# One core of a Trainium2: scales, rotated key and latents prepared in the merge, a query and key stage in a written order, and longer waits in the plan of a delta rule

## The chip, the cores and the metric

The kernel runs on one core of a Trainium2 chip. Its time is the device time of one execution in microseconds (us). A core has TensorE (PE, matrix products), VectorE (DVE), ScalarE (ACT), GpSimd (POOL) and SyncE (SP), each with a queue of its own that is worked off in order, and 16 DMA engines that move data between memory (HBM) and the core's SBUF. TensorE writes its products to PSUM.

## The reference

One layer of a diffusion trunk over 1024 tokens of width 1024 and 256 context tokens. A projection `h @ w_in` feeds three branches: a Fourier mix, a gated delta rule (4 heads, in both directions, in chunks) and attention with low-rank queries and keys (MLA, 8 heads); gates merge them. Cut to the parts that the change touches:

```python
# delta rule, one step of the scan over chunks
u_new = u_n - einsum('bhcd,bhde->bhce', w_n, S)
o = einsum(qg_n, S) + einsum(qk_n, u_new)
S = S * gl_n + einsum('bhcd,bhce->bhde', kd_n, u_new)
...
# MLA: 384 query latents cq, 256 key/value latents ckv, 32 key channels kpe
q = (rmsnorm(cq, q_norm) @ w_uq).reshape(B, L, 8, 64 + 32)
kv = (rmsnorm(ckv, kv_norm) @ w_ukv).reshape(B, L, 8, 64 + 64)
q_pe = apply_rope(q_pe, cos, sin);  kpe = apply_rope(kpe, cos, sin)
q = concatenate([q_nope, q_pe]);    k = concatenate([k_nope, k_pe for each head])
o = softmax(q @ k.T * 96 ** -0.5) @ v
...
merged = sum over a, b, c of sigmoid(g) * (y @ w_branch);  y = merged @ w_out
x = x + gate * rmsnorm(y, g_post)
```

## The kernel before

Values are float32. Where TensorE needs them, an operand is split into a high and a low half (names ending in h and l, or hi and lo), and a product is three matmuls: high x high, low x high, high x low. ScalarE writes the high half, VectorE or POOL the low one.

The stages follow one another, with the times of the profiled execution: a prologue (0 to 155 us), the delta rule over the context (to 330), the Fourier branch (to 427), the delta rule over the tokens (`gdn_lat`, to 985), the merge (`merge_ab`: gates to 1047, then a loop over eight output blocks m to 1139), the query and key stage (`qkv`, 1139 to 1240), attention (`attend`, to 1491) and the end (`final`).

In `gdn_lat` a planner, `drive`, mixes three kinds of generators: `prep` (the inverse of a head's chunk matrices: the 16 x 16 blocks are inverted by a chain of VectorE products and reductions `tmp`, `N`, L746 and L748, stored to `zd` and loaded as `Z`), `scan` (eight steps per head with S, y and u) and *fillers*, which are projections that other stages need later (`mm<-hhi,wh` and the like). A chain that yields a number says for how many us, times PAD = 1.25, it will wait; the planner issues filler pieces of three matmuls until that time is up by its own costs. With `self.fine` set, matmuls stay in the order in which the code issues them. Small functions put on `self.later` run inside a filler: `mla_scales` (the tokens' inverse norms, stored as `rkd` and `aqd`) and `rope_k` (the key channels `kped` times the table `ropek`, stored as `kpd`).

In the merge loop a block has 48 matmuls `pb` of 512 columns; VectorE multiplies them with gate values `t` (L1266). `ck_prep`, called after block 5, splits the key latents into `ckh`, `ckl` and the value weights into `wvh`, `wvl`. The gates' sum `gacc` runs over weights `in_wmod` that SP loads.

`qkv` computes from the latents: `k_tile(t)` and `qn_tile(t)` (keys and queries, PSUM tile `st`, stored by halves as `knh`, `knl`, `qnh`, `qnl`), `qp_tile` (rotated query channels, `qph`, `qpl`), `v_tile` (`acc`). Weights come by SP (`wr`, L209), are split into `wh` and `wl`. `load_k` and `load_q` bring the stored halves back as `K` and `Q` in the layout of attention. `peak` multiplies a tile of K and Q (`s`) and takes row maxima on VectorE (`mx`), which `shift` turns into the softmax's shift. The scheduler is free to interleave these.

Of the kernel before, what the change touches and what calls it, by code (L numbers as in the profile page):

```python
# [162 lines left out]
class K:  # L163
# [89 lines left out]
    def build(self):  # L253
        with ExitStack() as es:
# [27 lines left out]
            self.kpd = dr.tile([32, L], FP32, name="kpd")  # L282
# [38 lines left out]
            with tc.tile_pool(name="pre", bufs=1, side="right", reuse_waits="tile") as self.pre:  # L321
                self.merge_ab()
                esh.close()
                esq = ExitStack()
                self.qk = esq.enter_context(tc.tile_pool(name="qk", bufs=1, reuse_waits="tile"))
                self.pss = esq.enter_context(tc.tile_pool(name="pss", bufs=1, space=PSUM, reuse_waits="tile"))
                self.qkv()
            self.kq = es.enter_context(tc.tile_pool(name="kq", bufs=1, side="right", reuse_waits="tile"))
# [341 lines left out]
    def gdn_prep(self, kap, qap, gsl, bsl, h=0):  # L670
# [165 lines left out]
    def gdn_step(self, st, c, S, kap, ktok, vtok, M, bkc, eg, eL, lat, last, al):  # L836
# [129 lines left out]
    def gdn_lat(self):  # L966
# [16 lines left out]
        def scan(h, kT, qT, ktok, vtok, bk, M, Qf):  # L983
# [3 lines left out]
            for t in range(8):  # L987
# [7 lines left out]
                yield 0.8  # L995
# [45 lines left out]
    def fillers(self):  # L1041
# [3 lines left out]
        self.later.append(self.mla_scales)  # L1045
        self.later.append(self.rope_k)
# [57 lines left out]

    def mla_scales(self):
        nc, gp = self.nc, self.gp
        rk = gp.tile([P, 10], FP32, name="rk")
        nc.vector.tensor_scalar(out=rk, in0=self.ssk, scalar1=1.0 / 256, scalar2=EPS, op0=ALU.mult, op1=ALU.add)
        self.ipow(self.rkv, rk, -0.5)
        self.rkd = self.dram.tile([10, P], FP32, name="rkd")  # L1110
        nc.sync.dma_start(out=self.rkd.rearrange("t p -> p t"), in_=self.rkv, allow_slow_non_contiguous=True)
        rq = gp.tile([P, 8], FP32, name="rq")
        nc.vector.tensor_scalar(out=rq, in0=self.ssq, scalar1=96.0 / 384, scalar2=96 * EPS, op0=ALU.mult, op1=ALU.add)
        self.ipow(self.aq, rq, -0.5)
        self.aqd = self.dram.tile([8, P], FP32, name="aqd")
        nc.sync.dma_start(out=self.aqd.rearrange("t p -> p t"), in_=self.aq, allow_slow_non_contiguous=True)

    def rope_k(self):
        nc, gp = self.nc, self.gp

        def st():
            return gp.tile([P, 512], FP32, name="st", bufs=self.nb["st"])

        for b in range(0, L, 512):
            k, r, t = st(), st(), st()
            nc.sync.dma_start(out=k[0:64], in_=self.kped[:, b:b + 512])
            nc.sync.dma_start(out=r[0:64], in_=self.a["ropek"][:, b:b + 512])
            nc.gpsimd.tensor_tensor(out=k[0:64], in0=k[0:64], in1=r[0:64], op=ALU.mult)
            nc.scalar.copy(out=t[0:32], in_=k[32:64])
            nc.gpsimd.tensor_tensor(out=t[0:32], in0=t[0:32], in1=k[0:32], op=ALU.add)  # L1130
            nc.sync.dma_start(out=self.kpd[:, b:b + 512], in_=t[0:32])
# [85 lines left out]
    def merge_ab(self):  # L1217
        nc, tc, a = self.nc, self.tc, self.a
        with ExitStack() as es:
# [32 lines left out]
            for j in range(4, 8):  # L1252
                stage(j)
            acc = []
            for m in range(8):
# [17 lines left out]
                if m == 5:  # L1273
                    self.ck_prep(tile4)
# [7 lines left out]
    def ck_prep(self, tile4):  # L1282
        nc, pre = self.nc, self.pre
        self.ckh, self.ckl = (pre.tile([P, 2, LT], F32R, name=n) for n in ("ckh", "ckl"))
        row = self.rkd.rearrange("(o t) p -> o (t p)", o=1)
        for b, w in ((0, L), (L, LC)):
            rb = tile4()[:, 0:w]
            nc.sync.dma_start(out=rb, in_=row[:, b:b + w].broadcast_to([P, w]))
            for k in range(2):
                st = tile4()[:, 0:w]  # L1290
                nc.sync.dma_start(out=st, in_=self.ckvd[k][:, b:b + w])
                self.hilo(st, self.kvn[:, k:k + 1], rb, self.ckh[:, k, b:b + w], self.ckl[:, k, b:b + w])
        self.wvh, self.wvl = (pre.tile([P, 2, 512], F32R, name=n) for n in ("wvh", "wvl"))
        st = tile4().rearrange("p (k c) -> p k c", k=2)
        nc.sync.dma_start(out=st, in_=self.a["wuv"])
        self.split(st, self.wvh, self.wvl)

    def qkv(self):
# [6 lines left out]
        with ExitStack() as es:  # L1305
            up = es.enter_context(tc.tile_pool(name="up", bufs=1, side="right", reuse_waits="tile"))
            ckh, ckl = self.ckh, self.ckl

            def cst(w):
                return up.tile([P, LT], FP32, name="cst", bufs=3)[:, 0:w]  # L1310
# [8 lines left out]
            aqb = up.tile([P, L], FP32, name="aqb")  # L1319
            nc.sync.dma_start(out=aqb, in_=self.aqd.rearrange("(o t) p -> o (t p)", o=1).broadcast_to([P, L]))  # L1320
            rope = up.tile([P, 2, L], FP32, name="rope")
            nc.sync.dma_start(out=rope, in_=a["rope"])
            cqh, cql = (up.tile([P, 3, L], F32R, name=n) for n in ("cqh", "cql"))
# [9 lines left out]
            def k_pe():  # L1333
                kpe = cst(LT)[64:96]
                nc.sync.dma_start(out=kpe[:, 0:L], in_=self.kpd)
                nc.sync.dma_start(out=kpe[:, L:LT], in_=self.kped[0:32, L:LT])
                kh, kl = self.Kt[0]
                nc.scalar.copy(out=kh[64:96, 0], in_=kpe)
                nc.vector.tensor_tensor(out=kl[64:96, 0], in0=kpe, in1=kh[64:96, 0], op=ALU.subtract)
                nc.gpsimd.memset(kh[KR:KR + 1].bitcast(FP32), 1.0)  # L1340
                nc.sync.dma_start(out=self.Kt[1][0][KR:KR + 1].bitcast(FP32), in_=kh[KR:KR + 1].bitcast(FP32))
                for i in range(2):
                    src = self.Kt[0][i][64:KR, 0].bitcast(FP32)
                    for b, par in ((0, 1), (1, 0), (1, 1)):
                        nc.sync.dma_start(out=self.Kt[b][i][64:KR, par].bitcast(FP32), in_=src)
# [28 lines left out]
            k_pe()  # L1374
            for t in range(VF):
                v_tile(t)
            for t in range(4):
                k_tile(t)
                if t < 3:
                    st = cst(L)  # L1380
                    nc.sync.dma_start(out=st, in_=self.cqd[t])
                    self.hilo(st, self.qn_g[:, t:t + 1], aqb, cqh[:, t, :], cql[:, t, :])
            self.load_k(0)
            qn_tile(0)
            qp_tile(0)
            self.Qt = {}
            self.load_q(0)
            self.mx = {}
# [270 lines left out]
```

## Time and profile before

| | us |
|---|---|
| three runs | 1645.12, 1643.05, 1632.33 |
| their median | 1643.05 |
| the profiled execution | 1628.66 |
| its span, first to last instruction | 1626.9 |
| TensorE busy in it | 1519.6 |
| VectorE, ScalarE, POOL busy | 791.6, 544.6, 565.2 |

The profile is of one execution, which was 14.4 us shorter than the median of the runs. A busy TensorE is not TensorE at its peak: the granted clock has two levels, and a matmul of 512 columns takes 0.39 us from its start to its end at the full one, with starts 0.23 us apart.

### The profile page before, as it was taken

How to read it: one execution, taken by the hardware profiler on the slowest of the kernel's cores; microseconds unless marked ns; L12 is line 12 of the kernel's file. 1: busy time of each engine (PE TensorE's matmuls, PEld its weight loads, DVE VectorE, ACT ScalarE, POOL GpSimd, SP SyncE). 2: the span in 40 equal slices, each digit the busy share in tenths (PEclk: the TensorE clock that was granted, in tenths of full speed). 3: DMA queues.
4: the chain of work that ended last, by engine and by line, in shares of the span. 5: the costliest groups of instructions: out<-in, count | busy, mean ns of one | idle time of the engine just before them, and what ended most of it. 6: DMA issues, size and time to landing. Idle time of an engine off the chain costs nothing.

```text
span 1626.9 us, 20197 instructions
## 1 busy us (share of the span) xinstructions
PE 1519.6 (93%) x7401; PEld 1188.4 (73%) x7401; DVE 791.6 (49%) x1483; ACT 544.6 (33%) x1156; POOL 565.2 (35%) x466
## 2 busy tenths in 40 slices
PE   6888999999899969999999999999778998999998
PEld 1676788888788758878878888887555665656886
DVE  2755665453343235455255221523356765766724
ACT  3454324322322423343333332311322443443311
POOL 0364242221325434424424222243103665654000
PEclk9889999999999989999999999999888999999999
DMA  8511222312332223223223224655794122103715
GB/s 317 164 56 66 87 70 87 120 45 66 116 114 72 56 60 107 85 81 109 77 72 111 72 72 140 210 174 171 234 290 133 41 64 59 27 13 119 227 41 178
DMA packets 95211, 178.95 MB, mean 110 GB/s; under 512 B 23796, under 2 KB 28772, under 8 KB 94856
## 3 DMA queue, kind: packets, MB, share of 16 engines
q1 hardware_dynamic: 84328, 158.76, 31.7%
q10 hardware_dynamic: 10784, 18.91, 3.2%
q8 instruction: 58, 0.95, 0.2%
q14 instruction: 41, 0.34, 0.1%
HBM read 124.42 MB, written 52.18 MB: 109 GB/s over the span
## 4 chain that ended last, share of the span: by engine, by line
PE 70%; DMA 6%; DVE 6%; POOL 2%; issue 2%; ACT 1%; SPq 1%; POOLq 0%; DVEq 0%; ACTq 0%
PE mm L175 32%; PE st L175 9%; PE pp L175 7%; PE pf L175 5%; PE g L175 5%; PE pb L175 4%; PE acc L175 3%; PE pm L175 2%; PE s L175 2%; DVE tmp L746 1%; DMA Q<-sh 1%; DMA Z<-zd 1%; PE g L182 1%; DMA cst<-cqd 1%; SPq L733 1%
## 5 line engine op out<-in xcount | busy, mean ns | idle before, releaser
L197 POOL TENSOR_TENSOR wl<-wr,wh 128x512 fp32r<-128x512 f32 x142 | 194.4, 1371 | 547.6 <-ACT wh L196 536.1
L175 PE MATMUL mm<-hhi,wh 128*128 128x512 f32 x912 | 377.2, 414 | 1.4 <-ACT st L1077 1.0
L175 PE MATMUL mm<-hhi,wl 128*128 128x512 f32 x912 | 362.9, 398 | 0.0
L175 PE MATMUL mm<-hlo,wh 128*128 128x512 f32 x912 | 360.7, 395 | 0.0
L175 PEld LDWEIGHTS mm<-hhi,wl 128*128 128x128 f32 x912 | 173.6, 190 | 38.4
L175 PEld LDWEIGHTS mm<-hhi,wh 128*128 128x128 f32 x912 | 174.6, 191 | 33.3 <-ACT st L1077 1.4
L175 PEld LDWEIGHTS mm<-hlo,wh 128*128 128x128 f32 x912 | 174.7, 192 | 32.0 <-issue 0.5
L196 ACT CAST wh<-wr 128x512 fp32r<-128x512 f32 (+2 forms) x154 | 93.4, 609 | 244.7 <-PE mm L175 114.9
L175 PE MATMUL st<-Q,K 96*128 96x512 f32 (+1 forms) x480 | 139.9, 408 | 7.1 <-DMA Q<-sh 6.4
L1474 ACT ACTIVATE pf<-st 128x512 f32<-128x512 f32 x160 | 94.6, 596 | 128.3 <-PE st L175 125.6
L175 PEld LDWEIGHTS st<-Q,K 96*128 96x128 f32 (+1 forms) x480 | 89.3, 194 | 42.5 <-DMA Q<-sh 10.3
L1483 POOL TENSOR_TENSOR sum<-sum,pf 128x512 f32<-128x512 f32 x94 | 117.6, 1278 | 4.0 <-ACT pf L1474 3.8
L1435 DVE TENSOR_REDUCE mx<-s 128x1 f32<-128x512 f32 x128 | 86.7, 690 | 58.5 <-PE s L175 58.4
L175 PE MATMUL acc<-pf,V 128*64 128x512 f32 x320 | 72.2, 597 | 0.0
L175 PE MATMUL s<-K,Q 96*128 96x512 f32 (+1 forms) x192 | 63.5, 371 | 3.7 <-DVE mx L1435 3.3
L1077 ACT ACTIVATE st<-mm 128x512 f32<-128x512 f32 x56 | 33.3, 595 | 57.2 <-PE mm L175 55.2
L175 PEld LDWEIGHTS acc<-pf,V 128*64 128x64 f32 x320 | 21.6, 136 | 42.1 <-issue 42.1
L869 DVE SCALAR_TENSOR_TENSOR S<-S,ex,g 128x128 f32<-128x128 f32 x48 | 14.8, 343 | 76.6 <-PE g L175 76.6
L175 PE MATMUL pb<-yh,wh 128*128 128x512 f32 x128 | 50.8, 396 | 0.0
L175 PE MATMUL pb<-yh,wl 128*128 128x512 f32 x128 | 50.6, 395 | 0.0
L175 PE MATMUL pb<-yl,wh 128*128 128x512 f32 x128 | 50.5, 395 | 0.0
L878 POOL TENSOR_TENSOR Qm<-mk,Qf 128x128 f32<-128x128 f32 x64 | 28.5, 466 | 57.6 <-PE g L175 56.6
(392 smaller groups left out, 2728.5 us busy)
## 6 DMA issues: line engine op xcount, KB each, us to landing
wr<-in_win SPq DMA_DIRECT2D x118, 256.0 KB, 2.8
wm<-in_wmod SPq DMA_DIRECT2D x16, 512.0 KB, 7.1
tabd<-st ACTq DMA_DIRECT2D x24, 256.0 KB, 2.1
wr<-in_wbr SPq DMA_DIRECT2D x24, 256.0 KB, 3.3
t<-tabd SPq DMA_DIRECT2D x12, 512.0 KB, 4.4
xt<-in_xT SPq DMA_DIRECT2D x8, 640.0 KB, 11.1
wm<-in_win SPq DMA_DIRECT2D x8, 512.0 KB, 3.7
kqd<-lk SPq DMA_DIRECT2D x8, 512.0 KB
```

The lines of the kernel that those rows point to most:

```text
L175: i = self.nc.tensor.matmul(out, lhsT, rhs, start=start, stop=stop)
L182: i = self.nc.tensor.transpose(out=out, in_=in_, identity=identity)
L196: nc.scalar.copy(out=hi, in_=raw)
L197: self.lo_eng.tensor_tensor(out=lo, in0=raw, in1=hi, op=ALU.subtract)
L733: nc.sync.dma_start(out=yd[b].rearrange("u r c -> r u c"), in_=Y[s, :, s])
L746: nc.vector.tensor_tensor(out=tv, in0=XX[:, i:i + 1, i + 1:16].broadcast_to([P, m, m]), in1=N[:, i + 1:16, i + 1:16].rearrange("p k j -> p ...
L869: nc.vector.scalar_tensor_tensor(out=Sn[:, dr], in0=S[:, dr], scalar=eL(dr), in1=sp[:, dr], op0=ALU.mult, op1=ALU.add)
L878: nc.gpsimd.tensor_tensor(out=Qm[:, dr], in0=self.mk[:, m_, :], in1=Qf[:, c[dr], :], op=ALU.mult)
L1077: nc.scalar.activation(out=st, in_=ps, func=AF.Tanh, scale=0.5)
L1435: self.pin(nc.vector.tensor_reduce(out=mx[:, i, c:c + 1], in_=ps, axis=AX.X, op=ALU.max))
L1474: nc.scalar.activation(out=pf, in_=ps, func=AF.Exp)
L1483: nc.gpsimd.tensor_tensor(out=out, in0=s[0], in1=pf, op=ALU.add)
```

## The change

`mla_scales` and `rope_k` no longer run inside the delta rule. A new generator, `latents`, does their work and that of `ck_prep`, and also splits the query latents into `cqh` and `cql`, which `qkv` did. The merge loop takes one piece of it after each block from m = 1 on. The scales are transposed by TensorE before their store; the rotated key is computed on VectorE and stored in halves (`kpd`) by ScalarE's queue, and `qkv` loads `kpd` straight into the eight K tiles. The new pool `lat` lies where `hhi` and `hlo` were. In `qkv`, `self.fine` is set, so that the matmuls and the maxima go in the order of the code. Three numbers in the delta rule's plan are raised; the first of them stands under `if YR:`, and YR is 0.

```diff
@@ gdn_prep, gdn_step, scan @@
             if YR:
-                yield (10.0 if h == 0 else 7.0) if hf == 0 else 1.0
+                yield (14.0 if h == 0 else 7.0) if hf == 0 else 1.0
...
             if self.fine:
-                yield 1.4
+                yield 1.8
...
-                yield 0.8
+                yield 1.4
@@ fillers @@
-        self.later.append(self.mla_scales)
-        self.later.append(self.rope_k)
...
@@ merge_ab @@
+            self.esh.close()
+            self.lp = self.esl.enter_context(tc.tile_pool(name="lat", bufs=1, reuse_waits="tile"))
+            pieces = self.latents()
             acc = []
             for m in range(8):
...
-                if m == 5:
-                    self.ck_prep(tile4)
+                if m:
+                    next(pieces)
...
+    def latents(self):
...
+        for ss, m, n in ((self.ssk, 1.0 / 256, 10), (self.ssq, 96.0 / 384, 8)):
+            r = lp.tile([P, 10], FP32, name="tsr", bufs=2)[:, 0:n]
+            nc.vector.tensor_scalar(out=r, in0=ss[:, 0:n], scalar1=m, scalar2=EPS if n == 10 else 96 * EPS, op0=ALU.mult,
+                                    op1=ALU.add)
+            self.ipow(r, r, -0.5)
+            ps = self.mm1([P, P])[0:n]
+            self.tr(out=ps, in_=r, identity=self.mk[:, MK_ID, :])
+            t = lp.tile([10, P], FP32, name="tst", bufs=2)[0:n]
+            nc.scalar.copy(out=t, in_=ps)
+            d = self.dram.tile([n, P], FP32, name=f"tsd{n}")
+            nc.sync.dma_start(out=d, in_=t)
+            rows.append(d.rearrange("(o t) p -> o (t p)", o=1))
+        yield
...
+                nc.vector.tensor_tensor(out=k, in0=k, in1=r, op=ALU.mult)
+                nc.vector.tensor_tensor(out=k[:, 0], in0=k[:, 0], in1=k[:, 1], op=ALU.add)
...
+            nc.scalar.dma_start(out=self.kpd[:, :, b:e], in_=hl.bitcast(FP32))
+        yield
...
+        self.cqh, self.cql = (lp.tile([P, 3, L], F32R, name=n) for n in ("cqh", "cql"))
...
+            nc.sync.dma_start(out=st, in_=self.cqd[t])
+            self.hilo(st, self.qn_g[:, t:t + 1], rb, self.cqh[:, t, :], self.cql[:, t, :])
...
@@ qkv @@
-            k_pe()
-            for t in range(VF):
-                v_tile(t)
-            for t in range(4):
-                k_tile(t)
...
-            self.load_k(0)
-            qn_tile(0)
-            qp_tile(0)
...
+            self.fine = True
+            k_tile(0)
+            qn_tile(0)
+            qp_tile(0)
+            k_pe()
+            for t in range(VF):
+                v_tile(t)
+                if t == 2:
+                    self.load_k(0)
+                    self.load_q(0)
+            peaks(2)
             for t in range(1, 4):
-                qn_tile(t)
+                k_tile(t)
                 peaks(3)
-            self.load_q(1)
+                if t == 1:
+                    self.load_q(1)
+                if t < 3:
+                    qn_tile(t)
+                    peaks(4 if t == 1 else 5)
+            self.shift(0)
+            qp_tile(1)
+            qn_tile(3)
             for t in range(VF, 10):
                 v_tile(t)
-                peaks(2)
-            peaks(3)
-            self.shift(0)
-            qp_tile(1)
+            self.fine = False
```

**SP's queue in the delta rule, head 0's inverse.** X and `yd` are the blocks on their way to the inversion, `zd` and `Z` its result; before:

```order
L756 DMA zd<-big 64x1024
L1126 DMA st<-kped 64x512
L1127 DMA st<-in_ropek 64x512
L209 DMA wr<-in_win 128x512
L759 DMA Z_4706<-zd 16x8x64
L1116 DMA aqd<-aq 128x8x1
L1126 DMA st<-kped 64x512
L1131 DMA kpd<-st 32x512
L1127 DMA st<-in_ropek 64x512
L759 DMA Z_4706<-zd 16x8x64 x3
L1131 DMA kpd<-st 32x512
L1088 DMA zcd<-st 128x512
```

and now:

```order
L756 DMA zd<-big 64x1024
L759 DMA Z_4675<-zd 16x8x64 x2
L1086 DMA zcd<-st 128x512
L759 DMA Z_4675<-zd 16x8x64 x6
L1086 DMA zcd<-st 128x512
L209 DMA wr<-in_win 128x512 x2
```

Seven transfers between the store of `zd` and the loads of Z are gone, among them the 128x8x1 store of `aq`; two of the `zcd` stores that came behind the loads now stand among them.

**VectorE at the end of the inversion's chain, same head.** `tmp` and `N` are the chain, S is the scan's state, `oacc` its output, `big` the inverse on its way to `zd`; before:

```order
L746 TENSOR_TENSOR tmp_4397<-XX_4391,N_4394 128x196
L748 TENSOR_REDUCE N_4394<-tmp_4397 128x14
L869 SCALAR_TENSOR_TENSOR S<-S,ex,g 128x128
L746 TENSOR_TENSOR tmp_4397<-XX_4391,N_4394 128x225
L869 SCALAR_TENSOR_TENSOR S<-S,ex,g 128x128
L748 TENSOR_REDUCE N_4394<-tmp_4397 128x15
L893 TENSOR_TENSOR oacc<-g,oacc 128x128
```

and now:

```order
L746 TENSOR_TENSOR tmp_4397<-XX_4391,N_4394 128x196
L748 TENSOR_REDUCE N_4394<-tmp_4397 128x14
L746 TENSOR_TENSOR tmp_4397<-XX_4391,N_4394 128x225
L748 TENSOR_REDUCE N_4394<-tmp_4397 128x15
L751 COPY big<-N_4394 64x16x16
L753 COPY big<-N_4394 64x16x16
L869 SCALAR_TENSOR_TENSOR S<-S,ex,g 128x128 x2
L893 TENSOR_TENSOR oacc<-g,oacc 128x128
```

S was written in the last two rounds of the chain and is now written behind its copies to `big`.

**SP's queue in the query and key stage, first loads of K and Q and the next weights.** Before (the numbers behind K and Q are buffers):

```order
L1411 DMA K_9177<-knl 64x2x1280
L1354 DMA qnl<-csl 128x512 x2
L209 DMA wr<-in_wuq 128x384 x2
L1419 DMA Q_9562<-qnh 64x2x512
L1419 DMA Q_9563<-qnl 64x2x512
L209 DMA wr<-in_wuq 128x384 x2
L1419 DMA Q_9710<-qnh 64x2x512
L1419 DMA Q_9711<-qnl 64x2x512
```

and now, first the loads for the first peaks and then the weights of the second query tile:

```order
L1357 DMA K_9214<-kpd 32x1280 x2
L1424 DMA K_9211<-knh 64x2x1280
L1424 DMA K_9212<-knl 64x2x1280
L1432 DMA Q_9416<-qnh 64x2x512
L1433 DMA Q_9416<-qph 32x2x512
L1432 DMA Q_9417<-qnl 64x2x512
```

```order
L1432 DMA Q_9508<-qnl 64x2x512
L1366 DMA knl<-csl 128x512 x2
L1366 DMA knl<-csl 128x256
L1433 DMA Q_9508<-qpl 32x2x512
L209 DMA wr<-in_wuq 128x384
```

The loads `K<-kpd`, which were copies from K to K far ahead of this place, now stand in the row with the loads of K and Q, and the weights `wr<-in_wuq` of the second query tile behind the stores `knl` of the second key tile.

## Rows read from the trace of the kernel before

**Rows 1.** The page: busy time of TensorE, and the chain by engine.

```profile
PE 1519.6 (93%) x7401; PEld 1188.4 (73%) x7401; DVE 791.6 (49%) x1483; ACT 544.6 (33%) x1156; POOL 565.2 (35%) x466
...
PE 70%; DMA 6%; DVE 6%; POOL 2%; issue 2%; ACT 1%; SPq 1%; POOLq 0%; DVEq 0%; ACTq 0%
```

**Rows 2.** Busy us by stretch, as the first line names the columns.

```profile
core 0: us, PE busy (x) PEld busy (x) DVE busy (x) ACT busy (x) POOL busy (x), PEclk, DMA share, GB/s
427.00:990.00 563.00, 531.85 (x2902) 450.00 (x2902) 226.51 (x572) 193.61 (x530) 217.14 (x207) 0.98 0.29 89
590.00:610.00 20.00, 9.58 (x47) 8.19 (x46) 2.48 (x7) 3.17 (x9) 5.53 (x6) 0.76 0.24 40
1047.00:1139.00 92.00, 92.00 (x391) 72.28 (x390) 30.48 (x29) 12.02 (x19) 35.97 (x21) 1.00 0.55 174
1139.00:1240.00 101.00, 79.02 (x305) 59.70 (x304) 50.48 (x75) 29.66 (x52) 9.48 (x5) 0.86 0.80 243
1171.00:1190.00 19.00, 13.45 (x52) 9.51 (x50) 12.11 (x15) 7.07 (x12) 0.00 (x0) 0.91 1.00 325
1240.00:1255.00 15.00, 11.93 (x45) 8.89 (x45) 10.73 (x15) 7.73 (x13) 8.72 (x7) 0.89 0.44 144
```

**Rows 3.** Waits of TensorE, 416 to 990: us in total, times, longest.

```profile
PE g L175 <- ACT u L858: 10.4, 1, 10.4
PE g L175 <- DVE S L869: 6.3, 6, 2.5
PE g L175 <- DVE y L848: 5.5, 8, 1.3
```

**Rows 4.** Chain of waits, 580 to 612: start, us, what.

```profile
591.98 12.37 DMA Z<-zd
604.35 1.24 POOL st L1128
```

**Rows 5.** Timeline of SP, 588 to 612, and DMA of 586 to 606.

```profile
589.71 0.38 SPq L1116 DMA_DIRECT2D aqd<-aq  x1
...
591.98 1.52 SPq L759 DMA_DIRECT2D Z<-zd  x3
...
DMA packets 1862, 0.55 MB, mean 27 GB/s; under 512 B 1669, under 2 KB 1669, under 8 KB 1860
```

**Rows 6.** Timeline of TensorE: start, us, line, instruction, [idle before it].

```profile
578.43 0.49 PE L175 MATMUL g<-S,kT 128*128 128x128 f32 x2 [2.54 <-DVE S L869]
...
608.18 0.63 PE L175 MATMUL g<-S,qT 128*128 128x128 f32 x2
...
1160.19 0.39 PE L175 MATMUL st<-ckl,wh 128*128 128x512 f32 x1
1160.42 0.40 PE L175 MATMUL st<-ckh,wl 128*128 128x512 f32 x1
```

**Rows 7.** Waits of TensorE, 1100 to 1245.

```profile
PE st L175 <- ACT wh L196: 7.8, 1, 7.8
PE acc L175 <- ACT wvh L196: 4.8, 1, 4.8
PE st L175 <- DVE csl L1352: 3.8, 3, 2.0
```

**Rows 8.** Timeline of the query and key stage: SP, VectorE, TensorE.

```profile
1191.46 1.02 SPq L209 DMA_DIRECT2D wr<-in_wuq  x2
...
1207.63 0.69 DVE L1368 TENSOR_TENSOR cst<-st,rope 128x512 f32<-128x512 f32 x1 [1.40 <-PE st L175]
...
1217.42 0.67 PE L175 MATMUL s<-K,Q 96*128 96x512 f32 x2
```

**Rows 9.** Timeline of VectorE at the start of the merge.

```profile
1055.14 0.75 DVE L657 SCALAR_TENSOR_TENSOR gacc<-ys,sc,gacc 128x512 f32<-128x512 f32 x1 [0.83 <-DMA ys<-in_wmod]
1055.81 1.21 DVE L1266 SCALAR_TENSOR_TENSOR t<-t,pb 128x1024 f32<-128x1024 f32 x1
```

**Rows 10.** Groups by line, 1139 to 1240: busy us, mean ns, idle before.

```profile
L1435 DVE TENSOR_REDUCE mx<-s 128x1 f32<-128x512 f32 x16 | 10.6, 688 | 1.2 <-PE s L175 1.0
```

More of the change, by code (lines that the diff above doesn't have):

```diff
@@ L281, in build @@
             self.kped = dr.tile([64, LT], FP32, name="kped")
-            self.kpd = dr.tile([32, L], FP32, name="kpd")
+            self.kpd = dr.tile([32, 2, LT], FP32, name="kpd")
             esk = ExitStack()
@@ L1103, in spill_in @@
                     sums()
[L1105 to L1131, printed above, removed]
     def fourier(self):
@@ L1280, in hilo, with cs @@
         nc.vector.tensor_tensor(out=lo, in0=src, in1=hi, op=ALU.subtract)
[L1282 to L1285, printed above, removed]
+    def latents(self):
+        nc, lp = self.nc, self.lp
+        def cs(w):
+            return lp.tile([P, L], FP32, name="cs", bufs=3)[:, 0:w]
+        rows = []
+        for ss, m, n in ((self.ssk, 1.0 / 256, 10), (self.ssq, 96.0 / 384, 8)):
[11 more added lines that the diff above has]
+        yield
+        pieces = [(b, min(b + 512, LT)) for b in range(0, LT, 512)]
+        for b, e in pieces:
+            w = e - b
+            k = cs(2 * w)[0:32].rearrange("p (h c) -> p h c", h=2)
+            if b < L:
+                nc.sync.dma_start(out=k, in_=self.kped.rearrange("(h p) l -> p h l", p=32)[:, :, b:e])
+                r = cs(2 * w)[0:32].rearrange("p (h c) -> p h c", h=2)
+                nc.sync.dma_start(out=r, in_=self.a["ropek"].rearrange("(h p) l -> p h l", p=32)[:, :, b:e])
+                nc.vector.tensor_tensor(out=k, in0=k, in1=r, op=ALU.mult)
+                nc.vector.tensor_tensor(out=k[:, 0], in0=k[:, 0], in1=k[:, 1], op=ALU.add)
+            else:
+                nc.sync.dma_start(out=k[:, 0], in_=self.kped[0:32, b:e])
+            hl = lp.tile([32, 2, 512], F32R, name="kphl", bufs=1)[:, :, 0:w]
+            nc.scalar.copy(out=hl[:, 0], in_=k[:, 0])
+            nc.vector.tensor_tensor(out=hl[:, 1], in0=k[:, 0], in1=hl[:, 0], op=ALU.subtract)
+            nc.scalar.dma_start(out=self.kpd[:, :, b:e], in_=hl.bitcast(FP32))
+        yield
+        self.ckh, self.ckl = (lp.tile([P, 2, LT], F32R, name=n) for n in ("ckh", "ckl"))
@@ L1286, in ck_prep @@
         for b, w in ((0, L), (L, LC)):
-            rb = tile4()[:, 0:w]
-            nc.sync.dma_start(out=rb, in_=row[:, b:b + w].broadcast_to([P, w]))
+            rb = cs(w)
+            nc.sync.dma_start(out=rb, in_=rows[0][:, b:b + w].broadcast_to([P, w]))
             for k in range(2):
-                st = tile4()[:, 0:w]
+                st = cs(w)
                 nc.sync.dma_start(out=st, in_=self.ckvd[k][:, b:b + w])
                 self.hilo(st, self.kvn[:, k:k + 1], rb, self.ckh[:, k, b:b + w], self.ckl[:, k, b:b + w])
-        self.wvh, self.wvl = (pre.tile([P, 2, 512], F32R, name=n) for n in ("wvh", "wvl"))
@@ L1294, in ck_prep @@
-        st = tile4().rearrange("p (k c) -> p k c", k=2)
+            yield
+        self.cqh, self.cql = (lp.tile([P, 3, L], F32R, name=n) for n in ("cqh", "cql"))
+        rb = cs(L)
+        nc.sync.dma_start(out=rb, in_=rows[1].broadcast_to([P, L]))
+        for t in range(3):
+            st = cs(L)
+            nc.sync.dma_start(out=st, in_=self.cqd[t])
+            self.hilo(st, self.qn_g[:, t:t + 1], rb, self.cqh[:, t, :], self.cql[:, t, :])
+            if t == 0:
+                yield
@@ L1295, in ck_prep @@
+        yield
+        self.wvh, self.wvl = (lp.tile([P, 2, 512], F32R, name=n) for n in ("wvh", "wvl"))
+        st = cs(L).rearrange("p (k c) -> p k c", k=2)
         nc.sync.dma_start(out=st, in_=self.a["wuv"])
         self.split(st, self.wvh, self.wvl)
+        yield
     def qkv(self):
@@ L1333, in k_pe @@
             def k_pe():
[L1334 to L1345, printed above, removed]
+                row = self.Kt[0][0][KR:KR + 1].bitcast(FP32)
+                nc.gpsimd.memset(row, 1.0)
+                nc.sync.dma_start(out=self.Kt[1][0][KR:KR + 1].bitcast(FP32), in_=row)
+                for b in range(2):
+                    for i in range(2):
+                        for par in range(2):
+                            nc.sync.dma_start(out=self.Kt[b][i][64:KR, par].bitcast(FP32), in_=self.kpd[:, i])
             def put(f, dst, c):
@@ L1373, in qkv @@
             self.lo_eng = nc.vector
[L1374 to L1388 removed]
+            self.Qt, self.mx = {}, {}
             n = 0
```

19 lines of the change are left out of this document (8 added, 11 removed).

## Prediction

> **What bounds the kernel now.** I read the page first, then the chain of waits, then TensorE stage by stage, then its waits. TensorE (PE) is busy 93% of the span, and it holds 70% of the chain that ends last [rows 1]. An edit therefore pays only where PE stands idle or runs at half clock, and costs only where it makes it do so. The table by stretch [rows 2] shows where that is. In the delta rule (427 to 985 us) PE is busy 531.9 of 563 us; in the merge (1047 to 1139) it is busy all 92 us; in the query and key stage (1139 to 1240) only 79.0 of 101 us at a granted clock of 0.86. The change touches these three stages. The rest of the kernel keeps its order of instructions, so I give it nothing.
>
> **Part 1: scales and rotated key leave the delta rule.** PE idles 31 us in the delta rule (563 - 531.9), and one wait alone is 10.4 us: the matmul g<-u,ktok of the state's update waits for ScalarE's u [rows 3]. The chain of waits tells why [rows 4]: 12.37 us for the last loads of the inverse blocks Z, then the POOL multiplication of the rotated key, then ScalarE, whose copy for the rotated key stood ahead of u in its queue. The queue of SP shows what was issued just ahead of these loads: the store of aq, an array of 128 x 8 written with its axes exchanged and so in 1024 pieces of four bytes, then a load of kped, the store of a piece of rotated key and a load of ropek, and only then Z [rows 5]. From 586 to 606 us the DMA engines handle 1862 packets, 1669 of them under 512 bytes, at 27 GB/s. Both removed functions sit in this place: the store of aq, two loads, two stores, three pairs of POOL and ScalarE steps. In the new order of SP nothing stands between the Z loads but stores of zcd, so the 10.4 us go. The clock goes with them: in 590 to 610 us it was 0.76 over 9.58 us of busy PE [rows 2], or 2.3 us; after the stall the matmuls take 0.63 us where 0.39 is usual [rows 6]. I take 1.8 back. Sum: **-12.2**, bounds -8 (if Z still lands late behind the zcd stores) to -13. The other of these functions' small stores, that of the key's scales, caused no wait of PE, so its removal is worth nothing.
>
> **Part 2: longer waits in the plan.** The 10.0 made 14.0 changes nothing, since it stands under a constant that is 0. The two others put one more filler piece (three matmuls, 0.7 us at 0.232 us each) before S·kT and before y·M in each step. The waits that they can cover are those for S, 6.3 us in 6 times, and for y, 5.5 us in 8 [rows 3]. At most 14 x 0.7 = 9.8 us could go. But the longest, 2.54 us [rows 6], has another cause: VectorE works through the inversion's chain of 30 products and reductions in turn, and in the written order S stands at that chain's end, before as after. A piece of 0.7 us takes 2.5 to 1.8, not to 0. I take a third of the 11.8 us, **-3.8**; with bounds 0 (the chain moves along with the step) and -11.8. What would it cost? Work that a filler does earlier is not done later; after the last step 24 of its pieces are left where 87 were, so the supply doesn't run out.
>
> **Part 3: the merge takes the preparation on.** New in it are the scales, the rotated key on VectorE, cq's two halves and the split of wuv; ckv was there partly. VectorE is busy 30.5 of the 92 us, ScalarE 12, POOL 36 [rows 2]. Three cq pieces of about 1.28 + 1.22 us, the rotated key and the rest add some 13 us on VectorE, which stays under half. New bytes: cq 1.6 MB, two scale broadcasts net 0.5, rotated key 0.9, wuv 0.5, and rope 1.0 just ahead: 4.5 MB on 16 MB, DMA share .55 to about .70. No engine fills up. What is tight is the first block: the last step of the gates' sum gacc starts at 1055.14, after a wait of 0.83 for its weights, and the block's first product, which needs the whole sum, takes from 1055.81 to 1057.02 [rows 9]. It empties a PSUM buffer that PE wants for the second block 11.1 us (48 matmuls of 0.232) after the merge's first matmul at 1047.6, so at 1058.7; that leaves 1.7 us of slack. SP now issues the rope load ahead of gacc's weights and puts three branch-weight loads among them. A branch-weight load waits for a free buffer, and holds the sum's next weights back as long. I take **+2.5** with the clock that follows; bounds 0 and +5.
>
> **Part 4: the query and key stage in a written order.** Its matmuls are the same: 268 of 512 columns, 0.232 us apart [rows 6], and 32 half as long: 66 us. The stage takes 101, and the first 15 us of attention lose 3.1 us of idle PE and 1.3 of clock [rows 2]; so 39 us are there to win. Idle are 22 us, and the granted clock of 0.86 is worth 79.0 x 0.14 = 11. The waits by cause [rows 7]: 7.8 for wh, since the next weights were issued at 1191.46, behind two stores of qnl [rows 8]; 4.8 for wvh; 3.8 for csl; 8 for all others. The wait for wvh and, among the others, those for its low half and for cq (8 in all) go with the preparation in the merge. Attention gets 78 matmuls (18 us) between the last peak and its start, which covers the shift: -4.4.
>
> New or kept waits, in the new order:
> - The first peaks. From the last rotation product of the first query pair (1207.63) to the first peak (1217.42) it took 9.8 us [rows 8]. Six v tiles (8.4 us) now stand between, but SP has eight kpd loads and two K loads to issue ahead of the last Q loads, at 0.6 to 1.1 us each and with landings of 3.6 to 7.9. I take 5 (bounds 2 and 9).
> - Weights of the second query tile: their load stands behind the three stores of knl, as it did behind qnl. I take 5; bounds 0 and 7.8.
> - Peaks stand three to five in a row. VectorE needs 0.69 us for one [rows 10], PE 0.23: 20 x 0.46 = 9 us of idle PE, where before other matmuls lay between. Bounds 4 and 9.
> - csl: 2. Clock after the three longer waits: 1.7 each, near the 1.8 of part 1, so 5.
>
> 66 + 5 + 5 + 9 + 2 + 5 = 92 us in place of 101 + 4 = 105: **-13**. With all bounds low the stage takes 66 + 2 + 0 + 4 + 2 + 4 = 78 (-27), with all high 66 + 9 + 7.8 + 9 + 4 + 7 = 103 (-2).
>
> Is DMA a floor under this? The stage moves 24.5 MB (243 GB/s x 101 us) at a share of .80; in the stretch with the share at 1.00 it moves 325 GB/s [rows 2]. After the change some 4 MB less are moved in it: 20.5 MB / 325 GB/s = 63 us, and 84 us at the present mean of 243. So my 92 stands above the floor, but a stage of PE's 66 us alone would have no room for late landings, and I leave the low end at 78. The Trainium skill, "DMA: Bandwidth & Descriptors", section "Issuing engines are not separate DMA queues", says that transfers of all issuing engines share the same 16 DMA engines, and that another issuer saves only issue time. By that rule the 63 to 84 us hold whoever issues. By the opposite reading the stores of high halves, which ScalarE's queue issues, would not count, the floor would fall under PE's 66 us, and the low end would be 66 and 4 for the peaks, 8 us lower. The share of 1.00 with both queues at work bears the rule out, so the low end stays.
>
> **Sum.** -12.2 - 3.8 + 2.5 - 13 = **-26.5 us**. The profiled execution took 1628.66 us (span 1626.9), 14.4 below the median of the runs, 1643.05. Against itself the sum gives 1602; against the median 1616.5. I forecast **1616**: the median stands for the kernel, the one execution for itself.
>
> **Rivals.**
> 1. *The written order pays as much as it saves.* Freely mixed, the stage hid DVE's work behind other matmuls; written out, each wait is met in turn. For it: 20 peaks at 0.46 us and round trips of 9.8 us. Against: the 8 us for wvh, its low half and cq need no order to go. Then -12.2 - 3.8 + 2.5 = -13.5: 1629.5. Chance 0.2.
> 2. *Slower: weights behind stores.* Each up-projection tile's weights are loaded by SP, behind the stores of the tile before. If all seven after the first three come late by 7.8 us and cost 2 of clock, the losses are 69 us in place of 33 (22 idle, 11 clock): +36 - 13.5 = +22, 1665. It decides from five such tiles on (5 x 9.8 = 49 against 33 + 13.5). Against it: two weight buffers run ahead, and the v tiles need none. Chance 0.07.
> 3. *The merge starves.* The four chains that share three buffers cs block SP's queue ahead of branch weights; PE loses 10 us more there: 1626. Against: SP has 11 us per block. Chance 0.1.
> 4. *The preparation was all that the stage lacked.* It goes down to its low end of 78 us, and the waits for S and y lose 7 in place of 3.8: -12.2 - 7 + 2.5 - 27 = -43.7, 1599. Chance 0.13.
> That the change doesn't do what it says holds for the 14.0 alone, and costs nothing.
>
> **How the numbers follow.** The forecast has 0.5. Two kernels can be told apart by about 1%, or 16 us: under 1626.6 is faster, over 1659.5 slower. Faster: 0.46 of the forecast's, all of the fourth's, a third of the first's, half of the third's: 0.71. Same: 0.21. Slower: 0.08, nearly all the second's. Range: 1592 (the fourth with 7 us more, half the distance of the two base times) to 1637 (the first with part 1 at its weaker bound and part 2 near nothing, -8 - 0.5 + 2.5 = -6).
>
> **What would show it.** Right: no wait of PE over 3 us in the delta rule, few packets under 512 bytes there; PE busy through the merge but for its first 15 us; a stage of 88 to 96 us with waits for K or Q, for wh and for mx. Wrong: a wait of 8 us for wh at more than two tiles; waits for wbr in the merge; S waits as long as before.

## The result and the profile after

The changed kernel takes 1606.66 us in the median of four runs, the kernel before 1638.68 in four; the ratio is 0.983 (95% interval 0.980 to 0.986). The profiled execution took 1606.86 us, its span is 1605.1 (1626.9 before). The profiled execution of the kernel before, 1628.66 us, was 10 us shorter than the median of its runs, and that of the changed kernel was at its median: so the stages below add up to 21.8 of the 32 us between the medians, and no profile shows where the other 10 lie.

By stage, worked out from the starts in TensorE's timelines (the last store of the Fourier branch, the first product `pb` of the merge, 0.75 us after the start of its last `yh,wh`, the first product `st<-Q,K` of attention, the end of the span):

| us | to the end of Fourier | delta rule and gates | merge | query and key stage | rest | span |
|---|---|---|---|---|---|---|
| before | 429.7 | 617.9 | 91.9 | 100.5 | 387.0 | 1626.9 |
| after | 426.6 | 588.0 | 101.9 | 103.5 | 385.1 | 1605.1 |

So the gain is one of 30 us in the delta rule; the merge gives 10 back, and the stage whose order was written out gives back 3 (within what this stage varies by, see below). The windows of the changed kernel, cut at the same places, answer to [rows 2]:

```profile
core 0: us, PE busy (x) PEld busy (x) DVE busy (x) ACT busy (x) POOL busy (x), PEclk, DMA share, GB/s
426.60:1014.60 588.00, 577.23 (x3136) 489.65 (x3137) 240.07 (x592) 213.13 (x561) 225.07 (x211) 0.99 0.32 102
1014.60:1116.60 102.00, 94.42 (x392) 73.26 (x391) 49.11 (x50) 18.66 (x31) 42.76 (x24) 0.98 0.63 209
1116.60:1220.00 103.40, 80.28 (x303) 61.73 (x302) 42.44 (x66) 24.52 (x47) 8.71 (x5) 0.85 0.69 202
```

The delta rule and the gates of the kernel before, and of no_plan below (the change without its two longer waits):

```profile
429.70:1047.60 617.90, 586.87 (x3137) 495.13 (x3138) 245.80 (x596) 213.19 (x564) 231.15 (x217) 0.98 0.32 98
```

```profile
429.00:1028.90 599.90, 582.02 (x3137) 491.98 (x3138) 241.48 (x592) 212.15 (x562) 223.12 (x211) 0.99 0.31 100
```

In the first window of the changed kernel PE idles 10.8 us, where before it idled 31. The waits of TensorE there, 416 to 990 us, answer to [rows 3]; the wait for u is gone, those for S and y have halved:

```profile
PE g L175 <- DVE S L869: 2.8, 4, 1.7
PE pp L175 <- DMA kT<-kqd: 2.7, 1, 2.7
PE pp L175 <- ACT R L683: 2.4, 3, 1.4
PE g L175 <- DVE y L848: 2.2, 3, 0.8
```

From 985 to 1250 us, merge and query and key stage ([rows 7] before):

```profile
PE s L175 <- DMA Q<-qph: 9.6, 1, 9.6
PE pb L175 <- DVE t L1239: 7.6, 4, 3.3
PE s L175 <- DVE mx L1448: 6.5, 5, 1.7
PE st L175 <- ACT wh L196: 4.0, 1, 4.0
```

In the merge, where PE was busy throughout before [rows 2], it now waits for VectorE's product of a block. The timelines of SP, VectorE and TensorE show one such place:

```profile
1055.02 1.07 SPq L1299 DMA_DIRECT2D cs<-ckvd  x2
...
1061.94 2.57 DVE L1251 SCALAR_TENSOR_TENSOR cs<-cs,cvec 128x1024 f32<-128x1024 f32 x2 [7.03 <-DMA cs<-ckvd]
1064.43 2.42 DVE L1253 TENSOR_TENSOR ckl<-cs,ckh 128x1024 fp32r<-128x1024 f32 x2
1066.77 1.21 DVE L1239 SCALAR_TENSOR_TENSOR t<-t,pb 128x1024 f32<-128x1024 f32 x1
...
1068.12 0.77 PE L175 MATMUL pb<-yh,wh 128*128 128x512 f32 x1 [3.34 <-DVE t L1239]
```

VectorE stood 7.03 us at a latent's step whose load, issued at 1055.02, had not landed; the block's product stood behind it in its queue, and PE behind that.

In the query and key stage the first peaks wait:

```profile
1137.09 1.81 SPq L1357 DMA_DIRECT2D K<-kpd  x3
1138.95 0.67 SPq L1424 DMA_DIRECT2D K<-knh  x1
1139.67 0.60 SPq L1424 DMA_DIRECT2D K<-knl  x1
1140.37 0.57 SPq L1432 DMA_DIRECT2D Q<-qnh  x1
1140.99 1.00 SPq L1433 DMA_DIRECT2D Q<-qph  x1
...
1150.95 1.22 PE L175 MATMUL s<-K,Q 96*128 96x512 f32 x2 [9.63 <-DMA Q<-qph]
1151.97 0.63 PE L175 MATMUL st<-ckh,wh 128*128 128x512 f32 x1
```

The loads of K and Q go out in one row of SP behind kpd's; behind the wait of 9.63 us the matmuls of 512 columns take 0.63 us, where 0.39 is usual. This is the lower of the clock's two levels, called half clock here.

### The profile page after: what moved, and what is told of

The parts are those of the page before. It is cut to its first block, busy times and chain, and to the rows that moved or that the text cites. A ratio compares the mean times of both kernels' runs of the same rounds, so it can differ in the third digit from the quotient of the medians.

```text
span 1605.1 us, 20192 instructions
## 1 busy us (share of the span) xinstructions
PE 1513.2 (94%) x7403; PEld 1185.2 (74%) x7403; DVE 794.1 (49%) x1489; ACT 545.1 (34%) x1158; POOL 564.4 (35%) x462
## 4 chain that ended last, share of the span: by engine, by line
PE 71%; DVE 6%; DMA 6%; issue 2%; ACT 2%; POOL 1%; SPq 1%; ACTq 0%; DVEq 0%; POOLq 0%
PE mm L175 31%; PE st L175 10%; PE pp L175 7%; PE pf L175 5%; PE g L175 5%; PE acc L175 4%; PE pb L175 3%; PE pm L175 2%; PE s L175 2%; DVE tmp L746 1%; DMA Q<-sh 1%; DMA ys<-in_wmod 1%; DMA Q<-qph 1%; PE g L182 1%; DVE N L748 1%
## 5 line engine op out<-in xcount | busy, mean ns | idle before, releaser
L175 PEld LDWEIGHTS s<-K,Q 96*128 96x128 f32 x192 | 36.7, 194 | 30.8 <-DVE mx L1448 11.1
L878 POOL TENSOR_TENSOR Qm<-mk,Qf 128x128 f32<-128x128 f32 x64 | 31.9, 519 | 69.0 <-PE g L175 67.1
```

The costliest lines, as they stand in the source:

```text
L175: i = self.nc.tensor.matmul(out, lhsT, rhs, start=start, stop=stop)
L878: nc.gpsimd.tensor_tensor(out=Qm[:, dr], in0=self.mk[:, m_, :], in1=Qf[:, c[dr], :], op=ALU.mult)
```

## The experiments

Each kernel was compared with runs of the kernel before on the same chip. Stage times are from the profiled execution, by the same places as above:

| kernel | ratio (95% interval) | median us | delta rule and gates | merge | query and key |
|---|---|---|---|---|---|
| plan_only | 0.987 (0.984 to 0.991) | 1612.11 | 595.0 | 91.9 | 102.5 |
| no_plan | 0.990 (0.987 to 0.993) | 1617.13 | 599.9 | 102.3 | 98.2 |
| late_key | 0.995 (0.993 to 0.997) | 1625.67 | 601.9 | 97.8 | 103.8 |
| late_scales | 0.990 (0.987 to 0.993) | 1616.45 | 598.8 | 91.6 | 102.7 |
| plan_late | 0.985 (0.981 to 0.989) | 1607.16 | 592.0 | 91.9 | 102.0 |
| key_out | 0.991 (0.988 to 0.994) | 1615.6 | 600.8 | 100.3 | 97.5 |
| old_order | 0.980 (0.976 to 0.984) | 1599.5 | 589.4 | 101.0 | 83.3 |
| early_k | 0.980 (0.976 to 0.984) | 1597.45 | 584.4 | 104.7 | 98.3 |
| spread | 0.973 (0.970 to 0.976) | 1595.4 | 588.1 | 101.7 | 87.1 |
| pipe_old | 0.974 (0.972 to 0.976) | 1596.8 | 588.5 | 98.9 | 87.2 |
| pipe_spread | 0.976 (0.975 to 0.978) | 1599.32 | 590.4 | 99.0 | 92.0 |
| ahead | 0.971 (0.968 to 0.975) | 1587.57 | 584.5 | 102.4 | 82.2 |

Each stage time is one execution's, and equal code doesn't take equal time. The query and key stage in one written order took 103.5, 98.2 and 97.5 us in three kernels (after, no_plan, key_out), and 100.5 to 103.8 in the five with the old stage. The delta rule and gates took 584.4 to 590.4 us in the seven kernels that share the change's (after, and old_order to ahead in the table), the merge 101.0 to 104.7 in the six that share its, and the part up to the end of Fourier, the same in all, 426.6 to 432.1 (438.5 in pipe_spread). So a difference of some 5 us in one stage is no result by itself.

**What made the stall, and what is the plan's share?** Four kernels take the parts of the delta rule's change one by one.

plan_only is the kernel before with the two waits alone:

```diff
-                yield 1.4
+                yield 1.8
...
-                yield 0.8
+                yield 1.4
```

> The kernel before with the two longer waits of the plan alone (1.8 and 1.4). Delta rule and gates became 30 us shorter with the whole change, where I had 16. Theory: half of it, some 14 us, is the plan's, by shorter waits for S and y and less half clock behind them. Two cases for the 10.4 us stall, since here both loads of ropek stand ahead of the four-byte store of aq: if the stall comes of a ropek load that stands behind that store, it goes as well, and the ratio to the kernel before is about 0.984; if it comes of Z behind that store, PE still waits about 10 us in one piece, ratio 0.991. Rival: the plan is worth 4 us or less, and the removal of the key and the scales gave the rest: 0.997.

no_plan is the changed kernel with these two lines taken back.

> The changed kernel with the two waits of the plan at their old values (1.4 and 0.8). Theory: the waits for S and y come back to some 10 us, with the half clock behind them, so 14 us more than the changed kernel: ratio to the kernel before 0.991 to 0.992. Rival: the plan is worth 4 us or less: 0.986.

late_key is the kernel before with `rope_k` called at the fillers' end, and late_scales the same with the other, `mla_scales`:

```diff
         self.later.append(self.mla_scales)
-        self.later.append(self.rope_k)
...
                 yield from self.spill_in(M_G + 8 * b + m, 1, self.tabd[2 * m + b:2 * m + b + 1], "tanh")
+        self.rope_k()
```

> The kernel before with the rotated key computed at the end of the delta rule, the four-byte store of aq left in its place ahead of six of the eight Z loads. Theory: the stall needs both, the store and a POOL and ScalarE step that waits for a load behind it while u stands behind that step on ScalarE; with the key gone from there Z is late (10 us from issue to landing) but PE doesn't wait over 3 us: 12 us less, ratio 0.992. Rival: late Z alone makes PE wait: a wait of 8 to 10 us stays, ratio 0.998 to 1.0.

> The kernel before with the scales computed at the end of the fillers; the store of aq then stands behind all loads of Z, and the rotated key stays in its place. Theory (both are needed): the loads of ropek land in about 3 us, POOL and ScalarE go on, no wait of PE over 3 us: 12 us less, ratio 0.992. Rival: the loads of the key themselves (128 KB each) and the POOL steps make the stall: it stays at 5 us or more, ratio 0.996 to 1.0.

All four lose the wait of 10.4 us. The ratio of plan_only (0.987) lies between its two cases, 0.984 and 0.991, but the stall is gone, as in the first of them; no_plan and late_scales came out as their theories had it, within the intervals. In late_key the store of aq still stands ahead of six loads of Z, and Z is late. SP's timeline, and the rows of the tile Z:

```profile
592.00 0.38 SPq L1116 DMA_DIRECT2D aqd<-aq  x1
592.43 1.05 SPq L759 DMA_DIRECT2D Z<-zd  x2
...
595.23 1.87 SPq L759 DMA_DIRECT2D Z<-zd  x4
```

```profile
DMA to landing us min/median/max: 1.9/2.3/9.3
```

VectorE's timeline:

```profile
605.95 0.35 DVE L768 TENSOR_SCALAR R<-Z,par 128x256 f32<-128x256 f32 x1 [2.42 <-DMA Z<-zd]
```

A load takes 9.3 us where 2.3 is the median, VectorE waits 2.42, and PE has no wait for Z or u there. In late_scales the key's loads go without the store ahead of them. POOL's multiplication of the key's second piece, which waited 12.57 us in the kernel before (first line), has no wait (second line); that of the first piece waits 2.88 us, as it did before (2.92).

```profile
604.33 1.25 POOL L1128 TENSOR_TENSOR st<-st 64x512 f32<-64x512 f32 x1 [12.57 <-DMA Z<-zd]
```

```profile
592.72 1.28 POOL L1128 TENSOR_TENSOR st<-st 64x512 f32<-64x512 f32 x1
```

The profile of the kernel before puts the 12.57 us down to Z, but this step reads kped and ropek and not Z. What it waited for is most likely the load of ropek, issued behind the same store. So the stall needed both: a store in four-byte pieces ahead of a load on SP's queue, and steps on POOL and ScalarE that waited for that load with u behind them. Taking either away ends it. late_key missed its expected ratio (0.995 for 0.992), since its merge is 6 us longer: the gates' sum comes late there, and PE waits 4.4 us for the first block's product.

The share of the plan is 599.9 - 588.0 = 11.9 us (no_plan against after), that of the removal 617.9 - 599.9 = 18.0, each give or take the 5 us above. The ratios bear the plan's share out: 0.990 without it and 0.983 with it, with intervals that don't touch. In the plan's share PE's idle time falls from 17.9 to 10.8 us; the rest is PE's busy time for the same matmuls (582.0 to 577.2), put down here to half clock. The timeline of TensorE in no_plan, at the inversion's end:

```profile
577.31 0.49 PE L175 MATMUL g<-S,kT 128*128 128x128 f32 x2 [2.54 <-DVE S L869]
...
579.11 0.63 PE L175 MATMUL mm<-hhi,wh 128*128 128x512 f32 x1
579.54 0.63 PE L175 MATMUL mm<-hlo,wh 128*128 128x512 f32 x1
```

and in the changed kernel, at the same place, where no matmul of 0.63 us follows:

```profile
576.26 0.75 PE L175 MATMUL g<-S,kT 128*128 128x128 f32 x4 [1.65 <-DVE S L869]
```

**Do the two add up?** plan_late is plan_only with mla_scales at the fillers' end as well.

> The kernel before with the two longer waits of the plan and with the scales (and so the four-byte store) at the end of the fillers; merge and the query and key stage as before. Theory: the delta rule's 30 us are kept, and the 8 us that the merge and the stage lost together with the change are not paid: ratio 0.980 to 0.981, as fast as the changed kernel or faster. Rival: the two parts cover the same waits, since the plan alone took the stall away too: 0.987, as with the plan alone.

It lies between theory and rival and the interval holds neither out; by stages it keeps 25.9 of the 30 us, 3 more than plan_only, which by itself does not tell the two apart. plan_only had lost the stall too, since there both loads of ropek are issued ahead of the store of aq (SP's queue). The two parts overlap: 18.0 and 22.9 alone, 29.9 together.

**What does the merge pay for?** key_out is the changed kernel with the rotated key made on POOL and ScalarE at the fillers' end (a function like rope_k that stores the halves), and without the key's piece in `latents`.

> The changed kernel with the rotated key made at the end of the delta rule's fillers on POOL and ScalarE, and not in the merge. In the merge PE waits 7.6 us for the block's product on VectorE, 4 times. Theory: two or three of these are the rotated key's steps on VectorE, which wait for loads and stand ahead of the product; without them 3 to 4 us remain (the sum gacc and the loads of ckv), 4 to 6 us less in all: ratio 0.980. Rival: late gate sums and loads make these waits anyway: 6 us or more of waits, ratio 0.983.

In the merge the rival was right: it takes 100.3 us and PE still waits 6.6 there. The ratio, 0.991, missed both cases, since the moved work found another queue. TensorE's waits in the gates, and ScalarE's timeline:

```profile
PE mm L175 <- ACT t L1214: 9.1, 1, 9.1
```

```profile
995.12 0.40 ACT L1278 CAST st<-st 32x256 fp32r<-32x256 f32 x1 [4.13 <-DMA st<-kped]
995.43 1.06 ACT L1214 ACTIVATE t<-mm 128x512 f32<-128x512 f32 x2
```

TensorE waits for a tanh on ScalarE that stands behind copies and casts of the key; the last cast waits 4.13 us for its load, and a copy ahead of it 3.68 for POOL. It is a stall of the same kind as in the kernel before, in another place.

**What is the written order worth?** old_order is the changed kernel with the query and key stage as before (free, v tiles and key tiles first), and the preparation in the merge.

```diff
-            self.fine = True
-            k_tile(0)
-            qn_tile(0)
-            qp_tile(0)
             k_pe()
             for t in range(VF):
                 v_tile(t)
...
+            for t in range(4):
+                k_tile(t)
+            self.load_k(0)
+            qn_tile(0)
...
-            self.fine = False
```

> The changed kernel with the query and key stage in the order of the kernel before, free for the scheduler; the preparation stays in the merge. The stage took 103 us with the change where it took 100 before, though the waits for wvh, its low half and cq (8 us) are gone. Theory (the first rival of the prediction): the written order costs what the preparation saves, so the stage falls to about 90 and the kernel by some 11 us: ratio to the kernel before 0.976. Rival: the preparation saved nothing, since other waits took the place of these, and the order is neutral: stage 100 or more, ratio 0.982 or above.

The stage takes 83.3 us, 20 less than with the written order and 17 less than before. With the other kernels of each kind (pipe_old below has this order too and takes 87.2), the preparation was worth 13 to 20 us in this stage and the written order cost 10 to 20: most or all of it. Windows of the stage in old_order, spread and ahead (the last two below):

```profile
1121.15:1204.50 83.35, 71.89 (x303) 55.73 (x302) 38.42 (x62) 23.50 (x45) 5.05 (x3) 0.95 0.75 234
```

```profile
1117.85:1204.90 87.05, 72.41 (x303) 57.10 (x302) 41.48 (x66) 24.32 (x47) 8.71 (x5) 0.90 0.81 240
```

```profile
1116.25:1198.40 82.15, 71.48 (x303) 55.91 (x302) 42.08 (x66) 24.55 (x47) 9.66 (x5) 0.96 0.84 254
```

Against 80.28 us of busy PE at a clock of 0.85 after the change: 8 of the 20 us are busy time for the same matmuls, that is half clock. The whole time shows less than the stage does: 0.980 lies between theory and rival, its interval (0.976 to 0.984) overlaps that of the change (0.980 to 0.986), and the profiled execution, 1593.02 us, was the shortest of the four. That the written order costs time in all is clear from spread and ahead below, whose intervals end under 0.980.

Three kernels mend the written order step by step. early_k issues the loads of K ahead, and four of the eight of kpd (`k_load(b)` holds four):

```diff
...
             qn_tile(0)
+            k_pe()
+            k_load(0)
+            self.load_k(0)
             qp_tile(0)
-            k_pe()
             for t in range(VF):
                 v_tile(t)
                 if t == 2:
-                    self.load_k(0)
                     self.load_q(0)
+            k_load(1)
```

> The changed kernel with four of the kpd loads and the loads of K issued ahead of the first rotated query tile's stores, and the other four kpd loads behind the loads of Q. Theory: the wait for the first peaks (9.6 us) is SP's row of loads ahead of Q and falls to 5 us or less, with less half clock behind: 6 us less than the changed kernel, ratio 0.979 to 0.980. Rival: the round trip of the rotated query itself (9.8 us before) sets it; the wait stays above 8 us, ratio 0.983.

TensorE's waits in the stage:

```profile
PE st L175 <- ACT wh L196: 7.4, 1, 7.4
PE s L175 <- DMA Q<-qph: 2.4, 1, 2.4
```

The wait for Q falls to 2.4 us, as the theory has it, but the wait for the second query tile's weights grows from 4.0 to 7.4, and the clock stays at 0.86. The ratio's interval (0.976 to 0.984) holds theory and rival. spread puts the peaks between the tiles' parts (one behind each part of a key tile, two behind each of a query tile):

```diff
-                k_tile(t)
-                peaks(3)
+                k_tile(t, 1)
...
-                    qn_tile(t)
-                    peaks(4 if t == 1 else 5)
+                    qn_tile(t, 2)
...
```

> As early_k, and the peaks not three to five in a row but one behind each 512 columns of a key tile and two behind each of a query tile. In early_k the stage took 98.5 us with a granted clock of 0.86; in old_order 83.5 with 0.95. Theory: the written order lost by peaks in a row, paced by VectorE at 0.69 us each, and by the half clock behind these gaps; spread, the waits for mx (9 us with those at the end) fall to 3, the clock rises above 0.9, and the stage takes 88 us or less: ratio 0.973 to 0.976. Rival: what the written order loses is weights that come late behind stores, and mx waits only fill these gaps: the stage stays above 94, ratio 0.979.

The theory held: the waits for the maxima fall from 9.1 us to 2.9, those for mx alone to 1.3, and the stage to 87.1 at a clock of 0.90. One long wait is left, for weights behind the stores of knl:

```profile
PE st L175 <- ACT wh L196: 9.7, 1, 9.7
```

ahead loads an up-projection tile's weights two tiles early:

```diff
...
             def up_tile(wsrc, kt, rh, rl, w):
-                hi, lo = self.wload(wsrc, kt)
+                load_w()
+                hi, lo = ws.pop(0)
...
```

> As spread, and the weights of an up-projection tile are loaded two tiles ahead, so that those of the second query tile are issued before the v tiles and no longer behind the stores of the second key tile's low halves. In spread PE waits 9.7 us for them, at half clock for some us after. Theory: this wait goes to 1 us or less, the stage falls from 87 to 77 or less, and the kernel to a ratio of 0.966 to 0.968 to the one before, less than both kernels of the comparison. Rival: the loads of K and Q and the stores share the DMA engines at a share of 0.81, and something else comes late in its place (Q, K or the stores' buffers csl): the stage stays above 84, ratio 0.972 to 0.975.

```profile
PE s L175 <- DMA Q<-qph: 3.7, 1, 3.7
PE st L175 <- ACT wh L196: 2.8, 2, 2.4
```

The weights' waits fall to 2.8 us in two, but the first peaks' wait is 3.7 for 1.5: the stage gives 5 of the 10 us expected, 82.2. That and the ratio of 0.971 lie between theory and rival. The kernel's median is the lowest of all, 1587.57 us; its interval (0.968 to 0.975) overlaps that of spread (0.970 to 0.976).

**Loads a block ahead.** pipe_old and pipe_spread issue each load of `latents` one block before the step that uses it, with four buffers cs (old_order and spread otherwise):

```diff
+        x = key_in(0, 512)
         yield
+        key(0, 512, *x)
+        x = key_in(512, L)
+        yield
...
```

> As old_order, with the merge's preparation written so that each step's loads are issued one block ahead of the step that uses them, with four buffers in place of three. The merge takes 101 us with the preparation where it took 92 without. Theory: PE waits since VectorE, in order, stands at a preparation step whose load hasn't landed while the block's product stands behind it; with the loads a block ahead these waits (6.8 us) fall to 2 and the merge to 94 or 95: 6 us less than old_order, ratio 0.976. Rival: DMA share and POOL make the block slow whatever the order: merge 99 or more, ratio 0.980.

> spread and the pipelined merge together. If both theories hold the kernel is some 6 us faster than spread: ratio 0.970 to 0.972. If the merge's rival holds, as spread; if both rivals hold, 0.979.

The merge takes 98.9 and 99.0 us, 2 under the lowest of the six kernels with the change's merge. Of the waits for the block's product, 6.8 us in old_order, 3.9 are left in pipe_old, 2.95 of them in one wait behind the key's multiplication, which stands 4.64 us for its load of ropek. VectorE's and TensorE's timelines:

```profile
1038.94 1.21 DVE L1288 TENSOR_TENSOR cs<-cs 32x1024 f32<-32x1024 f32 x1 [4.64 <-DMA cs<-in_ropek]
1040.19 0.68 DVE L1289 TENSOR_TENSOR cs<-cs 32x512 f32<-32x512 f32 x1
1040.80 1.20 DVE L1239 SCALAR_TENSOR_TENSOR t<-t,pb 128x1024 f32<-128x1024 f32 x1
...
1042.15 0.47 PE L175 MATMUL pb<-yh,wh 128*128 128x512 f32 x1 [2.95 <-DVE t L1239]
```

That is a third of the 6 us expected. The ratios don't settle it: pipe_old has 0.974, even under its theory, but its profiled execution is 6 us longer than that of old_order (stage 87.2 for 83.3), and pipe_spread has 0.976 where spread has 0.973. pipe_spread's stage took 92.0 us for 87.1, with 2.9 us of waits for csl that spread has not, and its profiled execution lost 10.5 us ahead of the delta rule, in code that is the same; the runs show no cause for either.

## Why the prediction was right, point by point

The forecast of 1616 us, the direction and the range held, with luck: the mechanisms were mostly right, but none of the four terms had its size, and errors in opposite directions nearly cancelled. Against the profiled execution the sum was -26.5, and -21.8 is what it measured: -3.1 ahead of the delta rule and -1.9 behind the stage, where the code's order is unchanged and equal code varies by as much, and between them -29.9 + 10.1 + 3.0. Between the medians of the runs it is -32.0.

- **Part 1, -12.2.** The place was right, and so were the store, POOL and ScalarE in the chain; the load was not. The prediction took Z from the row of the wait, but in late_key Z is late and PE has no wait for u, and POOL's step reads ropek. It measured -18.0 (no_plan). The term was too small: with the stall of 10.4 us went 2.7 us of other waits (idle 31.0 to 17.9), and 4.9 us of busy time (586.9 to 582.0), where 1.8 were counted for half clock. The lower bound of -13 was broken.
- **Part 2, -3.8** (a third of 11.8 is 3.9). It measured -11.9, the low bound of -11.8. The step "takes 2.5 to 1.8, not to 0" was right for the wait (2.54 to 1.65), but PE's busy time, which fell by 4.8 us in all, was not counted, and the waits for S and y fell by more than a third, from 6.3 to 2.8 and from 4.9 to 2.2.
- **Part 3, +2.5.** It measured +10.1, twice the upper bound and the third rival's price, but not by its mechanism (PE has no wait for branch weights in the merge) nor mainly by the step that I named: the wait behind the sum gacc was 1.0 us. What failed is "no engine fills up": VectorE is busy 49 of 102 us, and still PE waits 7.6 us for it, since its queue is in order and stands at steps whose loads are late; busy PE is 94.4 us for 91.9 before, the other 2.6.
- **Part 4, -13.** It measured +3.0, and -1.9 behind the stage, where -4.4 of the -13 had been counted for the start of attention. The first rival happened: the written order cost most or all of what the preparation saved. Its waits were named rightly, first peaks 9.6 (5), weights 4.0 (5), maxima 9.1 (9), csl none (2); the step that failed is the clock, 5 us in the sum. Busy PE is 80.3 us against the 66 of the sum, 14 more. 5.5 of these stay even in ahead (71.5 at a clock of 0.96), so 66 was low too; the other 9 go with the slower clock of 0.85.
- **DMA as a floor.** In old_order and ahead the stage takes 82 to 83 us at 234 and 254 GB/s, inside the 63 to 84 us that were worked out; share .75 to .84. What remains there wasn't told apart further.
- **The signs.** In the delta rule no wait of PE is over 3 us, as forecast; packets under 512 bytes did not become few (1250 from 575 to 600 us, 1669 in 20 us before), so they were not the store's alone and did no harm by themselves. The merge's sign did not come, since PE waits there as late as 1068, 53 us into it, nor did the stage's 88 to 96 us. None of the signs of being wrong appeared.
- **The 14.0** changed nothing, since YR is 0; no run tried it alone.

## What to carry to other kernels

A step that waits for a load holds everything behind it on its engine's queue, however idle the engine is: before moving small work off one path, look at what will stand behind it on each queue of the new place (the key stalled the scan, then the gates, then the merge). An order written by hand should leave no row of matmuls that is paced by another engine and no weight load behind stores; here the same matmuls in the stage took 103 or 82 us. And count a wait of PE with the matmuls at half clock behind it: with the plan PE lost 7.1 us of idle time and 4.8 of busy time, and between the written and the old order of the stage 11.7 and 8.4. Last, a stage's time out of one execution is no measure of a few microseconds: equal code took times 5 us apart here.

## What the runs showed of the hardware

Behind a store of 1024 pieces of four bytes on the same queue a load of 32 KB took up to 9.3 us, where 2.3 is the median (late_key); with no such store ahead of these loads none whose landing the profile gives took over 2.7 (no_plan; 2.1 in plan_late). A wait of PE of 2.54 us was followed by matmuls of 0.63 us for 2 us and more, one of 1.65 us was not, at the same place of two kernels (no_plan and the changed one).
